# Hybrid decoder layer: the time mix's negated block inverse turned on VectorE, and output projection A taken by another order of column tiles

## The chip, the cores and the metric

One core of one Trainium2 chip runs the whole layer in one launch. The metric is the device time of one execution in microseconds. The kernel before took 2263.12 us (median of 3 runs, 2262.97 to 2263.64).

## What is computed

A sequence of 1040 tokens (16 learned meta tokens and 1024 inputs) of width 1024 goes through one layer:

```python
h = h + 0.5 * swiglu(rms_norm(h, ffn1_norm), ...)          # d_ff 2816
proj = rms_norm(h, mix_norm) @ w_in                        # q, k, v and the time mix's columns
sb = stick_breaking_attention(q, k, v)                     # 8 heads of 64
rw = rwkv7_time_mix(proj[..., 1536:], ...)                 # 8 heads of 64, a recurrence over tokens
h = h + concat([sb, rw]) @ w_out                           # the output projection
h = h + 0.5 * swiglu(rms_norm(h, ffn2_norm), ...)
out = rms_norm(h, final_norm)[:, 16:]
```

The time mix's state goes S <- S diag(w) - (S kk)(kk a)' + v k' from token to token, and a token's output is S r.

## The kernel before

**Tiles and groups.** Everything is kept transposed: channels on partitions, tokens along the free axis. The tokens are worked in two groups, A (16 meta tokens and 512 inputs) and B (512 inputs). Each fp32 operand is split into a high and a low fp32r part, and each product is three matmuls (high by high, high by low, low by high; `mm3`). A weight tile of 512 KB (eight blocks of 128 rows by 128 columns) is loaded by SyncE's queue (SP) into one of two buffers `wraw`. ScalarE (ACT) writes its high part `whi`, VectorE (DVE) its low part `wlo`, each with two buffers as well. So a tile can be split only when the tile two before it has been used up, and loaded only when the tile two before it has been split.

**The order of the work.** A planner written in the kernel (`Clock`) plays all tasks as generators against a model of the engines' costs. It issues each engine's instructions in the order in which its own clock would run them. The model counts 0.3 us of SP's time for a DMA. On the chip each engine runs its list in order, with semaphores, SP's list of DMAs too. The dense work (the FFNs and projections) is task 0 and runs through from end to end. The time mix's tasks (preparation, `lanes`, `chain`, `post`) and the attention's tasks are laid between its matmuls. Where the planner sees TensorE idle for longer than 0.45 us beside output projection A, it adds a pair of matmuls on the identity (`warm`).

**The time mix's inverse (`lanes`, line 1558).** The time mix goes by chunks of 64 tokens. There are eight units (two token groups, two halves of each, two pairs of heads), and one unit has 8 or 10 chunk and head pairs (Q). Each needs the inverse of a 64 by 64 unit triangular matrix per head and chunk. `lanes` first inverts the 16 by 16 diagonal blocks on GpSimd (POOL), one block on each partition. Its result T goes back to the matrices' layout through DRAM: one DMA `Td<-T`, and eight DMAs `t<-Td` of 8 or 10 KB that put block rows on partitions (tile t1, 128 partitions by Q by 32). A negated and turned copy goes the same way: ACT writes -T' to `lt`, one DMA writes it to Nd, and eight DMAs `tt<-Nd` put it on the diagonal of tt (128 partitions by Q by 128). Then TensorE merges 16 to 32 (matmuls `pw` and `pp`) and 32 to 64 (`pz` and `pe`). `pw` reads t1, `pp` reads tt. ACT and DVE carry the parts back into tt and t1. `chain` uses tt as the weights of `pu`.

**Output projection A (`wout`, line 2010).** It has eight column tiles m of 128 outputs and two ranges of 256 tokens, 0 and 1, hence sixteen products of 24 matmuls each. The order is given by `WOUT[0]` and a rule in `wout`: tiles 0 and 1 take both ranges; then tiles 2 to 7 take range 0; tiles 6 and 7 are kept and take range 1; then tiles 2 to 5 are loaded and split again and take range 1. It is twelve loads. Each product's result is added to the residual h on DVE, ACT squares it, and DVE adds the squares up. After the eighth product of range 0 its norm goes on (`norm_sums`, `norm_root`, `norm_end`): sums by TensorE (`nps`), a reciprocal root by DVE (`fst`), the root spread over the partitions by TensorE (`nyp`), and eight scaled and split blocks (`nf`, `nh`, `nl`) on DVE, ACT and POOL. FFN 2 begins with range 0's gate product (`pg`), which reads them. Range 1's norm follows while range 0 is in the first four gate and up products.

**The last range (`final_last`, line 2063).** The sums of the squares are matmuls too (`fss`). The loop transposes each tile into PSUM (`po`) as it is done. For the last tile (`hs`) it issues the sums of all squares but the last, then the two transposes of that tile, then the last square's sums, and then the root on DVE. DVE and ACT scale one half of the columns each (`ot`), and one DMA of 512 KB for each of two blocks of 128 tokens writes the output.

Of the kernel before, what the change touches and what calls it, by code (L numbers as in the profile page):

```python
# [7 lines left out]
F32 = mybir.dt.float32  # L8
F32R = mybir.dt.float32r
I32 = mybir.dt.int32  # L10
AF = mybir.ActivationFunctionType
# [5 lines left out]
P = 128  # L17
D = 1024
# [19 lines left out]
GB = 2  # L38
BUFS = [dict(raw=2, qs=4, kh=4, vs=2, sg=8, f=3, at=4, z=2, t=2, o=1),
        dict(raw=1, qs=4, kh=4, vs=2, sg=8, f=2, at=4, z=2, t=2, o=1)]  # L40
WOUT = ((0, 1, 2, 3, 4, 5, 6, 7, 2, 3, 4, 5), (0, 1, 2, 3, 4, 5, 6, 7))
QF = dict(ffn1=6, ffn2=4)
AHEAD = 0.1
IDLE = 0.45
# [430 lines left out]
class Ker:  # L475
# [1082 lines left out]
    def lanes(self, s, free):  # L1558


        nc, rp, dp = self.nc, self.rp, self.dp
        Q = 2 * s["NC"]
        nl, B = 8 * Q, 16
        ab = s["ab"]
        Ld, Td, Nd = (dp.tile([nl, B, B], F32, name=n, bufs=2) for n in ("Ld", "Td", "Nd"))
        blks = [(slice(B * i, B * i + B), slice(B * (i % 4), B * (i % 4) + B), slice(i * Q, i * Q + Q)) for i in range(8)]
        with self.urgent():
            for r, c, l in blks:
                nc.sync.dma_start(out=Ld[l].rearrange("l s t -> s l t"), in_=ab[r, :, c])
        yield from self.room(rp, ("lt", 1), ("T", 1), ("ltmp", 1))  # L1570
        lt = rp.tile([nl, B, B], F32, tag="lt", name="lt")
        T = rp.tile([nl, B, B], F32, tag="T", name="T")
        tmp = rp.tile([nl, 64], F32, tag="ltmp", name="ltmp")
        with self.urgent():
            nc.sync.dma_start(out=lt, in_=Ld)
        E = nc.gpsimd
        E.memset(T, 0.0)
        E.memset(T.rearrange("l i c -> l (i c)")[:, 0:B * B:B + 1], 1.0)
        for j in range(B - 1):
            m, w = B - 1 - j, j + 1  # L1580
            tv = tmp[:, 0:m * w].rearrange("l (i c) -> l i c", c=w)
            E.tensor_tensor(out=tv, in0=lt[:, j, j + 1:B].unsqueeze(2).to_broadcast([nl, m, w]),
                            in1=T[:, j, 0:w].unsqueeze(1).to_broadcast([nl, m, w]), op=ALU.mult)
            E.tensor_tensor(out=T[:, j + 1:B, 0:w], in0=T[:, j + 1:B, 0:w], in1=tv, op=ALU.subtract)
        nc.scalar.activation(lt.rearrange("l c i -> l i c"), T, AF.Copy, scale=-1.0)
        with self.urgent():
            nc.sync.dma_start(out=Td, in_=T)
            nc.sync.dma_start(out=Nd, in_=lt)
        yield lambda: free()
        yield self.after(T)  # L1590
        yield from self.room(rp, ("lr", 1), ("tt", 1), ("lw", 1))

        t1 = rp.tile([P, Q, 32], F32, tag="lr", name="t1")
        tt = rp.tile([P, Q, P], F32, tag="tt", bufs=1, name="tt")
        nc.gpsimd.memset(t1, 0.0)
        nc.gpsimd.memset(tt, 0.0)
        for r, c, l in blks:
            with self.urgent():
                nc.sync.dma_start(out=t1[r, :, r.start % 32:r.start % 32 + B], in_=Td[l].rearrange("l i c -> i l c"))
                nc.sync.dma_start(out=tt[r, :, r], in_=Nd[l].rearrange("l c i -> c l i"))  # L1600
        lw = rp.tile([P, Q * 48], F32, tag="lw", name="lw")
        w = lw[:, 0:16 * Q].rearrange("l (q i) -> l q i", i=16)
        z = lw[:, 16 * Q:48 * Q].rearrange("l (q i) -> l q i", i=32)
        g4 = [slice(32 * i, 32 * i + 32) for i in range(4)]
        up, dn = g4[0::2], g4[1::2]
        bank = (self.psc, "U", 2)
        mm = lambda out, l, r: nc.tensor.matmul(out, lhsT=l, rhs=r, start=True, stop=True)

        def U(nm, n):
            return self.psc.tile([P, 512], F32, tag="U", bufs=2, name=nm)[:, 0:n * Q].rearrange("p (q t) -> p q t", t=n)  # L1610

        yield self.need(t1, ab, bank=bank)
        pw = U("pw", 16)
        for c in range(Q):
            for i, g in enumerate(g4):
                mm(pw[g, c, :], ab[g, c, 32 * (i % 2):32 * (i % 2) + 32], t1[g, c, 0:16])
        nc.scalar.activation(w, pw, AF.Copy)
        yield self.need(w, tt, bank=bank)
        pp = U("pp", 32)
        for c in range(Q):  # L1620
            for i, g in enumerate(g4):
                mm(pp[g.start:g.start + 16, c, 0:16], w[g, c, :], tt[g, c, g.start + 16:g.stop])
        for c in range(Q):
            for g in up:
                mm(pp[g, c, 16:32], tt[g, c, g], w[g, c, :])
        for g in up:
            nc.vector.scalar_tensor_tensor(t1[g, :, 0:16], pp[g, :, 16:32], self.half[g], t1[g, :, 0:16], ALU.mult, ALU.add)
        for g in g4:
            nc.scalar.activation(tt[g.start:g.start + 16, :, g.start + 16:g.stop], pp[g.start:g.start + 16, :, 0:16], AF.Copy, scale=-1.0)

        yield self.need(t1, bank=bank)
        pz = U("pz", 32)
        for c in range(Q):
            for h in range(2):
                mm(pz[dn[h], c, :], ab[up[h], c, 32:64], t1[up[h], c, :])
        for h in range(2):
            nc.scalar.activation(z[dn[h]], pz[dn[h]], AF.Copy)
        yield self.need(z[dn[0]], z[dn[1]], tt, bank=bank)
        pe = U("pe", 32)
        for c in range(Q):  # L1640
            for h in range(2):
                mm(pe[up[h], c, :], z[dn[h], c, :], tt[dn[h], c, dn[h]])
        for h in range(2):
            nc.scalar.activation(tt[up[h], :, dn[h]], pe[up[h]], AF.Copy, scale=-1.0)
        s["tt"] = tt
# [364 lines left out]
    def wout(self, h2, n, hook, ready=None, late=False):  # L2010


        nc = self.nc
        ow = self.wcols("w_out")

        def one(m, wh, wl, i):
            cs = slice(256 * i, 256 * i + 256)
            if ready:
                yield lambda: ready(i)
            yield self.need(*[x[k][:, cs] for k in range(KT) for x in n[0:2]], bank=self.nextbank)  # L2020
            pd = self.bank("pwo")[:, 0:256]
            for k in range(KT):
                self.mm3(pd, wh[:, k, :], wl[:, k, :], n[0][k][:, cs], n[1][k][:, cs], k == 0, k == KT - 1)
                yield
            hd = h2[:, m, cs]
            with self.urgent():
                nc.vector.tensor_tensor(out=hd, in0=pd, in1=hd, op=ALU.add)
            hook(i, m)
        load = lambda m, keep=False: self.wget(ow[:, :, m * P:m * P + P], KT, P, keep)
        kept = []  # L2030
        for j, m in enumerate(WOUT[late]):
            keep = m > 5 and not late
            w = yield from load(m, keep)
            for i in (0, 1) if m < 2 or late else (int(j > 7),):
                yield from one(m, *w, i)
            if keep:
                kept.append((m, w))
            if keep and m == 7:
                for q, x in kept:
                    yield from one(q, *x, 1)  # L2040
                    self.drop(x)
# [21 lines left out]
    def final_last(self, s, h2, cs, bank, early):  # L2063
# [3 lines left out]
        for m in range(KT):  # L2067
            yield lambda: s()["k"] > min(max(m, m // 4 * 6), KT - 1)
            if m == KT - 1:
                sums = self.norm_sums(s(), 256, "fss", bank)  # L2070
                for _ in s()["last"]:
                    yield next(sums)
                last = next(sums)
                src = s()["scaled"]
            else:
                src = h2[:, m, cs]
            yield self.need(src)
            for b in range(2):
                if m % 4 == 0:
                    if m:  # L2080
                        yield self.need(bank=self.nextbank)
                    pts.append((bank if m else early)("po"))
                    self.hold(pts[-1:])
            for b in range(2):
                nc.tensor.transpose(out=pts[m // 4 * 2 + b][:, m % 4 * P:m % 4 * P + P], in_=src[:, b * P:b * P + P],
                                    identity=self.ident)
        yield last
        st, _ = yield from sums
        yield lambda: hasattr(self, "fo")
        for b in range(2):  # L2090
            ot = self.fo.tile([P, D], F32, name="ot%d" % b)
            with self.urgent():
                nc.vector.tensor_scalar(out=ot[:, 0:512], in0=pts[b], scalar1=st[:, 1, b:b + 1], scalar2=None, op0=ALU.mult)
                nc.scalar.activation(ot[:, 512:D], pts[2 + b], AF.Copy, scale=st[:, 1, b:b + 1])
                nc.sync.dma_start(out=self.out[0, 512 + cs.start + b * P:512 + cs.start + b * P + P, :], in_=ot)
        self.drop(pts)


# [435 lines left out]
```

## Time and profile before

| | |
|---|---|
| median of 3 runs | 2263.12 us |
| the profiled execution's own time | 2261.24 us |
| its span (first to last instruction) | 2259.5 us |
| TensorE busy, of the span | 2231.0 us, 99% |
| VectorE, ScalarE, GpSimd busy | 68%, 49%, 25% |
| TensorE's mean granted clock | 0.997 |

The profile is one execution. PE is TensorE's matmuls, PEld its weight loads, SPq the queue of DMAs that SyncE issues. The time of an SPq row is its issue, with what it waited for, and not the transfer. Matmuls overlap: the start of the next one tells their rate, not the duration of one. A bracket at the end of a row is the engine's idle time before it, and what ended it. All instructions carry line 104, the helper that records them, so rows are told apart by their tiles.

### The profile page before, as it was taken

Reading aid. Unit: us, or ns where it says so; the run is one execution under the profiler, and the core shown is the slowest. Engines: PE = TensorE matmul, PEld = TensorE weight load, DVE = VectorE, ACT = ScalarE, POOL = GpSimd, SP = SyncE. Lnnn points to the kernel's source line nnn. Section 1 sums busy time; section 2 is a strip of 40 time slices with the busy share of each in tenths; the row PEclk is TensorE's granted clock in tenths of the full one; section 3 lists DMA queues with packets and bytes.
Section 4 is the critical chain, followed back from the end, with each engine's and each line's share of the span. In section 5 each row is a group of like instructions: output and inputs, shape, how many; then the busy total and the mean of one; then the engine's idle time right before and its main releaser. Section 6 shows DMA issues by size and latency. Waiting matters only on the chain.

```text
span 2259.5 us, 41743 instructions
## 1 busy us (share of the span) xinstructions
PE 2231.0 (99%) x16409; PEld 1979.1 (88%) x16409; DVE 1547.4 (68%) x2633; ACT 1096.6 (49%) x2176; POOL 567.8 (25%) x722
## 2 busy tenths in 40 slices
PE   9999999999999999999999989999999999999998
PEld 8999999999878888778788988887778899899998
DVE  5887776475766745666476888557776556897774
ACT  5444444534354434554434554535665435454444
POOL 1321111013233132542011424324444001221110
PEclk9999999999999999999999999999999999999999
DMA  5543332545643233322556534233222433333332
GB/s 171 176 113 103 89 99 78 171 132 139 189 115 98 78 96 112 92 78 82 167 147 179 150 100 124 77 111 99 85 78 68 141 107 126 108 97 109 103 93 76
DMA packets 408442, 257.61 MB, mean 114 GB/s; under 512 B 44973, under 2 KB 392325, under 8 KB 408246
## 3 DMA queue, kind: packets, MB, share of 16 engines
q1 hardware_dynamic: 408246, 254.95, 38.5%
q8 instruction: 129, 2.11, 0.4%
q14 instruction: 67, 0.55, 0.1%
HBM read 220.90 MB, written 33.99 MB: 113 GB/s over the span
## 4 chain that ended last, share of the span: by engine, by line
PE 95%; DVE 3%; ACT 1%; issue 1%; DMA 0%; DVEq 0%; ACTq 0%
PE pd L104 35%; PE pu L104 22%; PE pg L104 21%; PE pwo L104 3%; PE px L104 3%; PE po L104 2%; PE pz L104 2%; PE pat L104 2%; DVE wlo L104 1%; PE pG L104 1%; PE psw L104 0%; ACT whi L104 0%; DVE nl L104 0%; PE pp L104 0%; PE pT L104 0%
## 5 line engine op out<-in xcount | busy, mean ns | idle before, releaser
L104 ACT ACTIVATE whi<-wraw 128x1024 fp32r<-128x1024 f32 x314 | 330.5, 1053 | 318.8 <-PE pd L104 209.0
L104 DVE TENSOR_TENSOR wlo<-wraw,whi 128x1024 fp32r<-128x1024 f32 (+1 forms) x312 | 399.5, 1281 | 93.7 <-ACT whi L104 87.2
L104 PE MATMUL pd<-ah,whi 128*128 128x512 f32 (+2 forms) x944 | 327.2, 347 | 2.6 <-DVE h L104 1.8
L104 PE MATMUL pd<-ah,wlo 128*128 128x512 f32 (+2 forms) x944 | 319.1, 338 | 0.0
L104 PE MATMUL pd<-al,whi 128*128 128x512 f32 (+2 forms) x944 | 318.9, 338 | 0.2
L104 PE MATMUL pd<-nh,whi 128*128 128x256 f32 (+7 forms) x648 | 210.5, 325 | 0.0
L104 PE MATMUL pu<-nh,whi 128*128 128x512 f32 (+3 forms) x576 | 205.5, 357 | 0.1
L104 PE MATMUL pd<-nl,whi 128*128 128x256 f32 (+7 forms) x648 | 204.5, 316 | 0.0
L104 PE MATMUL pd<-nh,wlo 128*128 128x256 f32 (+7 forms) x648 | 204.5, 316 | 0.0
L104 PEld LDWEIGHTS pd<-ah,whi 128*128 128x128 f32 x944 | 177.6, 188 | 27.1 <-issue 4.4
L104 PE MATMUL pu<-nl,whi 128*128 128x512 f32 (+3 forms) x576 | 197.8, 343 | 0.0
L104 PE MATMUL pu<-nh,wlo 128*128 128x512 f32 (+3 forms) x576 | 197.7, 343 | 0.0
L104 PE MATMUL pg<-nh,whi 128*128 128x512 f32 (+3 forms) x536 | 196.3, 366 | 0.6 <-ACT nh L104 0.6
L104 PEld LDWEIGHTS pd<-ah,wlo 128*128 128x128 f32 x944 | 177.6, 188 | 20.5
L104 PEld LDWEIGHTS pd<-al,whi 128*128 128x128 f32 x944 | 177.8, 188 | 17.6 <-DVE al L104 1.1
L104 POOL TENSOR_TENSOR qs<-wraw 128x512 f32<-128x512 f32 x64 | 97.7, 1530 | 373.9 <-DVE ql L104 124.6
L104 PE MATMUL pg<-nl,whi 128*128 128x512 f32 (+3 forms) x536 | 188.6, 352 | 0.9 <-DVE nl L104 0.9
L104 PE MATMUL pg<-nh,wlo 128*128 128x512 f32 (+3 forms) x536 | 188.3, 351 | 0.0
L104 POOL TENSOR_TENSOR al<-sl,ah 128x512 fp32r<-128x512 f32 (+2 forms) x45 | 71.2, 1581 | 346.1 <-ACT ah L104 336.4
L104 DVE SCALAR_TENSOR_TENSOR h<-pd,h 128x256 f32<-128x256 f32 (+1 forms) x200 | 107.6, 542 | 73.7 <-PE pd L104 71.3
L104 PEld LDWEIGHTS pd<-nh,whi 128*128 128x128 f32 (+2 forms) x648 | 120.1, 185 | 12.4 <-issue 3.1
L104 PEld LDWEIGHTS pd<-nh,wlo 128*128 128x128 f32 (+2 forms) x648 | 120.1, 185 | 8.9 <-DVE wlo L104 0.2
(395 smaller groups left out, 5657.0 us busy)
## 6 DMA issues: line engine op xcount, KB each, us to landing
wraw<-in_ffn_w_gate_dram SPq DMA_DIRECT2D x90, 512.0 KB
wraw<-in_ffn_w_up_dram SPq DMA_DIRECT2D x90, 512.0 KB
wraw<-in_ffn_w_down_dram SPq DMA_DIRECT2D x88, 512.0 KB
wraw<-in_w_in_dram SPq DMA_DIRECT2D x54, 512.0 KB
wraw<-in_w_out_dram SPq DMA_DIRECT2D x20, 512.0 KB
s<-rkvd SPq DMA_DIRECT2D x18, 256.0 KB
raw<-qkvd SPq DMA_DIRECT2D x16, 264.0 KB
raw<-qkvd SPq DMA_DIRECT2D x16, 256.0 KB
```

The lines of the kernel that those rows point to most:

```text
L104: self._c.trace(self._n, op, lambda: f(*a, **k), out, [x for x in args if isinstance(x, bass.AP)], k)
```

## The change

Three parts. In `lanes`, -T' no longer goes by way of ACT, Nd and eight DMAs: when t1 has landed, one VectorE instruction transposes its 32 by 32 blocks into z (part of the tile `lw`), and four ACT instructions copy them, negated, onto the diagonal of tt. In output projection A, tiles 0 to 3 take both ranges at once, tiles 4 to 7 take range 0, tiles 6 and 7, kept, take range 1, and only tiles 4 and 5 are loaded again: ten loads. In `final_last`, all sums and the root are issued ahead of the last tile's two transposes, and each output block goes out in two DMAs of 256 KB.

```diff
-WOUT = ((0, 1, 2, 3, 4, 5, 6, 7, 2, 3, 4, 5), (0, 1, 2, 3, 4, 5, 6, 7))
+WOUT = ((0, 1, 2, 3, 4, 5, 6, 7, 4, 5), (0, 1, 2, 3, 4, 5, 6, 7))
...
-        Ld, Td, Nd = (dp.tile([nl, B, B], F32, name=n, bufs=2) for n in ("Ld", "Td", "Nd"))
+        Ld, Td = (dp.tile([nl, B, B], F32, name=n, bufs=2) for n in ("Ld", "Td"))
...
-        nc.scalar.activation(lt.rearrange("l c i -> l i c"), T, AF.Copy, scale=-1.0)
         with self.urgent():
             nc.sync.dma_start(out=Td, in_=T)
-            nc.sync.dma_start(out=Nd, in_=lt)
...
                 nc.sync.dma_start(out=t1[r, :, r.start % 32:r.start % 32 + B], in_=Td[l].rearrange("l i c -> i l c"))
-                nc.sync.dma_start(out=tt[r, :, r], in_=Nd[l].rearrange("l c i -> c l i"))
...
+        yield self.after(t1)
+        nc.vector.transpose(out=z, in_=t1)
+        for g in g4:
+            nc.scalar.activation(tt[g, :, g], z[g], AF.Copy, scale=-1.0)
         yield self.need(t1, ab, bank=bank)
...
-            for i in (0, 1) if m < 2 or late else (int(j > 7),):
+            for i in (0, 1) if m < 4 or late else (int(j > 7),):
...
                 sums = self.norm_sums(s(), 256, "fss", bank)
-                for _ in s()["last"]:
-                    yield next(sums)
-                last = next(sums)
+
+                st, _ = yield from sums
...
-        yield last
-        st, _ = yield from sums
...
-                nc.sync.dma_start(out=self.out[0, 512 + cs.start + b * P:512 + cs.start + b * P + P, :], in_=ot)
+                for c in (slice(512, D), slice(0, 512)):
+                    nc.sync.dma_start(out=self.out[0, 512 + cs.start + b * P:512 + cs.start + b * P + P, c], in_=ot[:, c])
```

## Rows read from the trace of the kernel before

**Rows 1.** Stretches: us, busy us (instructions) of PE, PEld, DVE, ACT, POOL, clock, DMA
```profile
1252.00:1323.00 71.00, 64.16 (x696) 60.86 (x695) 57.34 (x113) 39.16 (x82) 25.13 (x45) 0.95 0.50 138
2250.00:2259.50 9.50, 2.03 (x20) 1.94 (x18) 3.48 (x12) 1.68 (x3) 0.00 (x0) 0.73 0.28 110
```

**Rows 2.** PE's waits: who waited for whom, us in total, times, longest
```profile
PE pz L104 <- DVE t L104: 4.3, 2, 3.8
PE pu L104 <- ACT us L104: 2.0, 4, 0.8
PE pwo L104 <- DVE wlo L104: 1.2, 2, 0.8
```

**Rows 3.** PE in order of time, output projection A: start, us, instruction, idle before
```profile
1288.26 0.28 PE L104 MATMUL pwo<-nh,wlo 128*128 128x256 f32 x1
1304.28 0.38 PE L104 MATMUL warm<-ident 128*128 128x128 f32 x2
1308.49 0.24 PE L104 MATMUL pz<-t,ab 32*32 32x32 f32 x2 [3.83 <-DVE t L104]
1309.17 1.06 PE L104 MATMUL pz<-t,ab 32*32 32x32 f32 x30 [0.44 <-DVE t L104]
1310.16 0.58 PE L104 MATMUL pwo<-nh,whi 128*128 128x256 f32 x1
1311.45 0.58 PE L104 MATMUL pwo<-nh,wlo 128*128 128x256 f32 x1 [0.49 <-DVE wlo L104]
...
1315.67 0.31 PE L104 MATMUL pwo<-nh,whi 128*128 128x256 f32 x1
```

**Rows 4.** SP's queue in order of time, same stretch
```profile
1286.79 0.50 SPq L104 DMA_DIRECT2D Td<-T  x1
1290.27 0.46 SPq L104 DMA_DIRECT2D Nd<-lt  x1
1290.84 2.44 SPq L104 DMA_DIRECT2D t<-Td  x5
1293.39 2.25 SPq L104 DMA_DIRECT2D tt<-Nd  x5
1299.47 1.03 SPq L104 DMA_DIRECT2D wraw<-in_w_out_dram  x2
```

**Rows 5.** ACT in order of time, same stretch
```profile
1303.40 1.06 ACT L104 ACTIVATE whi<-wraw 128x1024 fp32r<-128x1024 f32 x1 [2.90 <-DMA wraw<-in_w_out_dram]
1304.37 0.70 ACT L104 ACTIVATE nh<-nf 128x256 fp32r<-128x256 f32 x2
```

**Rows 6.** POOL in order of time: the last block of range 0's norm
```profile
1308.37 0.72 POOL L104 TENSOR_TENSOR nl<-nf,nh 128x256 fp32r<-128x256 f32 x1 [0.81 <-ACT nh L104]
```

**Rows 7.** The chain of waits, output projection B
```profile
1798.41 44.10 PE pwo L104 x378
```

**Rows 8.** Tiles tt and lt: duration ns min/median/max, first and last start
```profile
L104 ACT ACTIVATE tt<-pe x16: 358/375/428, 558.1 to 1461.5; 32x256 f32<-32x256 f32 x12, 32x320 f32<-32x320 f32 x4
L104 ACT ACTIVATE lt<-T x8: 635/646/660, 535.0 to 1438.9; 64x256 f32<-64x256 f32 x6, 80x256 f32<-80x256 f32 x2
```

**Rows 9.** DVE in order of time: the nearest and the longest instructions of such a shape
```profile
2250.46 0.35 DVE L104 TENSOR_SCALAR hs<-h2B,vec 128x256 f32<-128x256 f32 x1
1290.77 1.23 DVE L104 TENSOR_TENSOR_SCAN pe<-dec,rst 128x520 f32<-128x520 f32 x1
```

**Rows 10.** The end, in order of time: PE, DVE, SP
```profile
2251.27 0.41 PE L104 MATMUL po<-ident,hs 128*128 128x128 f32 x2
2251.53 0.50 PE L104 MATMUL fss<-ones,nsq 128*128 128x1 f32 x4
2253.64 1.41 DVE L104 TENSOR_SCALAR ot<-po,fst 128x512 f32<-128x512 f32 x2
2254.47 0.99 SPq L104 DMA_DIRECT2D out_dram<-ot  x2
```

**Rows 11.** DMA rate from 2240 to 2260, in 40 slices of 0.5 us
```profile
GB/s 0 0 0 0 0 33 0 0 0 0 0 303 381 389 389 381 254 0 0 0 0 0 0 0 0 0 0 0 0 0 188 401 410 410 401 287 0 0 0 0
```

## The prediction

> **What bounds the kernel now.** I read the page's table of engines first: TensorE is busy for 2231.0 of 2259.5 us, at a mean clock of 0.997. The change removes no product of the dense work, so it can only win what is left: 28.5 us of idle time, and stretches at the low clock. Next the busy time by stretch. The end has 9.5 - 2.03 = 7.5 us of idle TensorE, and output projection A 71.0 - 64.16 = 6.8 us, the one long stretch with a clock below 1.00 [rows 1]. In the waits of TensorE the largest entry is `pz` for t1, 4.3 us, nearly all of it one wait of 3.8; weight splits (`pwo` for `wlo`) make 1.2 us [rows 2]. So I read that stretch in order of time, engine by engine.
>
> **What happens there.** TensorE runs out of work after the `warm` pair at 1304.28, stands for 3.83 us, then 0.44 and 0.49: 4.76 us [rows 3]. Behind that come matmuls at a slower rate. From 1310.16 to 1315.67 there are 21 of them in 5.51 - 0.49 = 5.02 us, 0.239 us each; output projection B, undisturbed, runs 378 in 44.10 us, 0.117 each [rows 3, 7]. This is TensorE's lower clock of 1.2 GHz, after it had stood. It costs 5.02 - 21 x 0.117 = 2.6 us there, and about 0.5 us in the 32 small `pz` before. The hole is worth 4.76 + 3.1 = 7.8 us.
>
> Its cause is in two queues. SP issues `Td<-T` at 1286.79, then stands until 1290.27 for ACT's turned copy (`Nd<-lt`), then issues eight `t<-Td` and eight `tt<-Nd`, about 0.47 us each; only at 1299.47 does the next load of w_out follow [rows 4]. ACT's next instruction is the split of that load: it stands 2.90 us, until 1303.40 [rows 5]. Behind it in ACT's list wait the blocks of range 0's norm, and the pieces of tt and t1 that `pz` needs. So `pz` waits for DVE, DVE for ACT, ACT for a load, and the load for SP's place behind the lanes.
>
> **The change, part by part.**
>
> *SP's queue in `lanes`.* Per unit, `Nd<-lt` and eight `tt<-Nd` go. By the rows just read: the stand at `Nd`, 1290.27 - 1286.79 - 0.50 = 3.0 us, its issue of 0.46, and 8 x 0.45 = 3.6, together 7.0 us [rows 4]. The load would be issued at 1292.5 instead of 1299.5 and land 3.9 us later (1303.40 - 1299.47), near 1296.4. Without its 2.90 us stand ACT would have been ready at 1300.5, so half of the 7.0 us would do. This alone should close the hole.
>
> *Order of the tiles.* Two of twelve loads go, with their splits on ACT (1.06 us each [rows 5]) and DVE. Tiles 0 to 3 now serve two products each, 2 x 24 x 0.117 = 5.6 us per load, so loads run ahead; the second loads of 4 and 5 are wanted when 6 and 7 of range 1 run, and their buffers come free with the splits of 6 and 7. Of the 1.2 us of `pwo` waits, 0.5 is in the hole; of the other 0.75 I count half, 0.4 (bounds 0 to 0.75).
>
> The same edit takes cover away. Between the last product of range 0 and its gate stand four products, no longer six. Range 0's norm took from 1288.54 (end of its last product) to 1309.09 (last `nl`), 20.6 us [rows 3, 6]. Of this ACT's stand and split took 2.90 + 1.06 = 4.0, leaving 16.6. Four products are 11.2 us of matmuls. The whole projection took 70 us for 16 x 2.8 = 44.8; less some 9.9 us of waits and low clock, other tasks make up a quarter of TensorE's time, so the four last 11.2 / 0.745 = 15.0 us. I take 16.6 - 15.0 = 1.6, as 1.5 us, a new idle wait at `pg`. Bounds: 0 (the eight steps of the root do not wait among the preparation's scans), and 20.6 - 15.0 = 5.6 us, with which the 3.1 us of low clock would come back: 8.7.
>
> *DVE and ACT in `lanes`.* Per unit one transpose of 128x256, and four copies of 32x256 with the stride of tt, 0.375 us each like `tt<-pe`, less one `lt` of 0.646: 0.85 us more on ACT [rows 8]. The trace has no such transpose. From both sides: 0.35 us (a 128x256 instruction) and 1.23 (a scan of 128x520) [rows 9]; I take 0.4, since the element count is that of the first. Eight units: 3 us more on DVE, 7 on ACT, both idle for a third or more of the span. The new wait is the transpose's for t1's eight DMAs. Behind it on DVE are weight splits, residual adds and `chain`'s copies, and TensorE's waits for such copies were 0.8 us at most [rows 2]. Before, `pw` waited for t1 and never idled for it. Per unit 0 to 0.8 us, in all 0 to 6.4; it could also gain, as tt is ready some 4 us sooner, but no TensorE wait names that. I take 0.5 us lost.
>
> The trace cannot price the transpose; the Trainium skill's "VectorE: DVE Perf Modes", section "The three transpose paths", gives 311 ns for 128x128 bf16. By its figure an estimate is about 0.6 us for twice the columns, and the sum above would not move.
>
> *The end.* The last sums stand behind the `po` of the last tile: they start at 2251.53, that pair at 2251.27; moved ahead they gain 0.26 us, and the pair then runs beside the root, which takes until 2253.64 [rows 10]. Four DMAs for two: the last issue moves back by about 0.5 us (0.99 for two [rows 10]), but has half the bytes. Four DMAs of 256 KB just before ran at 381 to 389 GB/s, two of 512 KB at 401 to 410 [rows 11]: 0.1 us more on 1 MB. In the end the transfer is bound by the rate, and I take -0.3 for both (bounds -0.5 and +0.5).
>
> Against this edit speaks the Trainium skill, "DMA: Bandwidth & Descriptors", "Rules for kernel authors": it wants at least 1 MiB per DMA for the full rate. The trace agrees in the sign, by that twentieth.
>
> *Elsewhere.* The planner's order changes from the first unit on (from about 520 us). The waits outside this stretch and the two ends sum to some 10 us in pieces below 1 us; I take 0, with ±2.
>
> **Sum.** -7.8 - 0.4 + 1.5 + 0.5 - 0.3 = -6.5 us. Against the profiled execution's 2261.24 (span 2259.5 and 1.7 around it) this is 2254.7. The median shown is 1.9 above that execution, so 2256.6.
>
> **Rivals.**
>
> *A load still stands behind the lanes.* SP still keeps `Td`, its round trip through DRAM and eight `t<-Td`, and loads still wait for free buffers in order. For it: SP stood at other things too in this stretch. Against it: half of the 7.0 us is enough. If half the hole stays: -6.5 + 3.9 = -2.6, 2260.5.
>
> *The norm takes the hole's place.* Four products do not cover it. At the full 20.6 us the loss is 8.7 instead of 1.5: -6.5 + 7.2 = +0.7, 2263.8. For it: DVE was busy for 57.3 of 71 us there [rows 1]. Against it: the 4.0 us for the load go.
>
> *All waits of the projection go.* No norm wait, no lanes' wait, and the smaller waits of the stretch (about 1.7 in all) go too: -7.8 - 1.7 - 0.3, and 1 us from elsewhere: -10.8, 2252.3.
>
> *Slower: DVE stands for t1.* The planner puts the transpose where its model has t1 landed, with no slack; it counts a small DMA at 0.3 us of SP's time, the rows show 0.47 [rows 4]. Eight of them make it late by 8 x 0.17 = 1.4 us, in each of eight units. With the transpose and the four copies in series behind it, 0.4 + 4 x 0.375 = 1.9 us, a unit's merges come up to 3.3 us later than planned, 8 x 3.3 = 26 us. If half of that reached TensorE, 13: -6.5 - 0.5 + 13 = +6.0, 2269.1. The time is worse than before from (6.5 + 0.5) / 8 = 0.9 us of TensorE's idle time per unit, and beyond what can be told from no change from 1.4. Against it: `pw`, which needs the same data, did not idle in any unit, and DVE is idle for a third of the span.
>
> **How the numbers follow.** What a measurement of this kernel can tell from no change is about 0.2%, 4.5 us: 2258.6 to 2267.6. The forecast 0.45 and all waits going 0.13 lie below it: faster 0.58. The half hole 0.12, the norm 0.12, and the planner's order eating 3 us or more 0.08 lie within: same 0.32. DVE standing, 0.10, lies above: slower 0.10. The range reaches from all waits going with 1 us more from elsewhere, 2251, to the norm case with a little, 2265; it leaves out about 0.15.
>
> **What would show it.** Right: SP's next load of w_out directly behind eight `t<-Td`; no wait of `pz` above 1 us; the clock 1.00 in all of projection A; ten loads of w_out there; a transpose near 0.4 us; `pg` with at most 2 us ahead of it; the last `fss` ahead of the last `po`. Wrong: a wait of over 4 us at `pg` with the clock falling behind it, or DVE idle ahead of its transposes with TensorE waits for `us` of over 1 us.

## The result, and the profile after

The changed kernel takes 2269.15 us (median of 10 runs, 2267.35 to 2273.26) against 2264.15 for the kernel before in the same set: a ratio of 1.0025, 95% interval 1.0017 to 1.0033. It is slower by 5.0 us where 6.5 us less were forecast, and above the range.

Its profiled execution took 2269.35 us, near its median. That of the kernel before, 2261.24, lay 2.9 us below the median just given, so the two traces differ by 3 us more than the kernels do.

The page after: span, and busy time, share and instructions of each engine.

```profile
span 2267.6 us, 41710 instructions
PE 2239.6 (99%) x16423; PEld 1985.3 (88%) x16423; DVE 1542.4 (68%) x2639; ACT 1103.0 (49%) x2198; POOL 571.5 (25%) x722
```

TensorE is busy for 8.6 us more, with the same dense work, and idle for 28.0 us as against 28.5. What is lost is hidden in busy time: matmuls at the low clock, and `warm` matmuls (48 for 34) that the planner puts where TensorE has nothing else.

The two stretches of [rows 1] after; a third, where the clock was 1.00 in the kernel before, and the same with what lies around it (from 1215); all of output projection A with what lies around it (to 1340); and what follows (to 1450). Then the last four of these stretches of the kernel before.

```profile
1252.00:1323.00 71.00, 65.79 (x697) 62.62 (x697) 50.65 (x111) 37.97 (x86) 27.66 (x46) 0.93 0.42 120
2250.00:2267.60 17.60, 10.39 (x92) 10.13 (x90) 6.49 (x24) 7.34 (x15) 0.00 (x0) 0.83 0.32 120
1240.00:1248.00 8.00, 6.73 (x43) 6.39 (x42) 5.55 (x13) 4.38 (x11) 0.00 (x0) 0.79 0.58 180
1215.00:1252.00 37.00, 35.60 (x411) 32.60 (x410) 30.52 (x63) 19.95 (x52) 4.53 (x5) 0.95 0.45 137
1252.00:1340.00 88.00, 82.11 (x837) 78.23 (x837) 65.65 (x153) 47.30 (x113) 27.66 (x46) 0.94 0.40 114
1340.00:1450.00 110.00, 106.32 (x856) 89.53 (x856) 82.26 (x160) 56.56 (x123) 54.96 (x94) 1.00 0.36 100
```

```profile
1240.00:1248.00 8.00, 7.39 (x66) 6.72 (x64) 5.85 (x16) 4.48 (x11) 0.54 (x1) 1.00 0.62 190
1215.00:1252.00 37.00, 35.96 (x341) 33.10 (x342) 31.47 (x66) 22.20 (x58) 5.05 (x6) 1.00 0.53 158
1252.00:1340.00 88.00, 80.35 (x835) 76.35 (x833) 71.92 (x154) 49.80 (x109) 26.97 (x47) 0.96 0.45 126
1340.00:1450.00 110.00, 107.58 (x909) 90.76 (x908) 82.31 (x158) 57.03 (x124) 51.81 (x92) 1.00 0.37 103
```

From such a row I take what TensorE lost: its idle time, and (1 - clock) of the stretch. The clock is given to 0.01, so such a loss is known to some 0.4 us in 88. From 1252 to 1340 that is 7.65 + 3.5 = 11.2 us before and 5.9 + 5.3 = 11.2 after. The hole's gain is not there. From 1240 to 1248 it is 0.6 before and 1.27 + 1.68 = 3.0 after; with the neighbourhood, 1215 to 1252, it is 1.0 and 3.2.

SP's queue after, beside [rows 4]: no stand at `Nd`, no `tt<-Nd`, and the next load of w_out directly behind eight `t<-Td`, 8.3 us behind `Td` and not 12.7, where 12.7 - 7.0 = 5.7 were forecast. Two `mixd<-yt` came in between: SP now stood 3.0 us (1290.31 to 1293.28) for `yt`, as it had stood for `Nd`.

```profile
1289.77 0.54 SPq L104 DMA_DIRECT2D Td<-T  x1
1293.28 0.81 SPq L104 DMA_DIRECT2D mixd<-yt  x2
1294.18 3.73 SPq L104 DMA_DIRECT2D t<-Td  x8
1298.02 0.40 SPq L104 DMA_DIRECT2D wraw<-in_w_out_dram  x1
```

DVE, ACT and then PE, each in order of time, in the same stretch. The transpose takes 0.45 us. Read the two splits of tile 4, which is loaded a second time: the high part at 1306.74, the low part at 1317.67.

```profile
1299.20 0.45 DVE L104 STREAM_TRANSPOSE lw<-t 128x256 f32<-128x256 f32 x1 [1.43 <-DMA t<-Td]
1305.11 0.34 DVE L104 SCALAR_TENSOR_TENSOR t<-pp,half,t 32x128 f32<-32x128 f32 x1 [2.45 <-ACT tt L104]
1306.16 0.42 DVE L104 TENSOR_TENSOR h<-pwo,h 128x256 f32<-128x256 f32 x1
1306.88 1.28 DVE L104 SCALAR_TENSOR_TENSOR nf<-h,vec,ny 128x256 f32<-128x256 f32 x3 [0.29 <-ACT ny L104]
...
1316.10 0.74 DVE L104 TENSOR_TENSOR nl<-nf,nh 128x256 fp32r<-128x256 f32 x1 [0.67 <-ACT nh L104]
...
1317.67 1.20 DVE L104 TENSOR_TENSOR wlo<-wraw,whi 128x1024 fp32r<-128x1024 f32 x1
```

```profile
1299.74 1.71 ACT L104 ACTIVATE tt<-lw 32x256 f32<-32x256 f32 x4 [1.47 <-DVE lw L104]
1306.74 1.05 ACT L104 ACTIVATE whi<-wraw 128x1024 fp32r<-128x1024 f32 x1
1313.03 1.06 ACT L104 ACTIVATE whi<-wraw 128x1024 fp32r<-128x1024 f32 x1 [1.54 <-PE pwo L104]
```

```profile
1306.64 0.58 PE L104 MATMUL pwo<-nh,whi 128*128 128x256 f32 x1 [1.58 <-DVE h L104]
1312.95 0.38 PE L104 MATMUL warm<-ident 128*128 128x128 f32 x2
1313.89 0.49 PE L104 MATMUL warm<-ident 128*128 128x128 f32 x2
1315.70 0.66 PE L104 MATMUL warm<-ident 128*128 128x128 f32 x4
1318.19 0.66 PE L104 MATMUL pu<-us,tt 128*128 128x64 f32 x4 [1.83 <-ACT tt L104]
1318.69 1.09 PE L104 MATMUL warm<-ident 128*128 128x128 f32 x6
```

The waits of [rows 3] are gone, and others stand in their place. Between the two splits DVE does the blocks of range 0's norm (`nf`, `nl`), which are urgent, while a load's split has one level less. The load of tile 4 was not what was late: it was issued at 1289.31, ahead of the lanes' DMAs. Behind a stand of 1.58 us (until 1306.64) TensorE finishes tile 7's product by 1313.1; then it has a little of the time mix, 14 `warm` (2.6 us) and a stand of 1.83 us, and the next product starts at 1319.4. With all `warm` of the stretch counted as idle (18 matmuls, 3.4 us; before 6, 1.15 us) it lost 14.6 us, and before 12.3: 2.2 us more.

The two traces differ by 8.1 us (spans 2267.6 and 2259.5). Of these 2.2 lie between 1215 and 1252, 2.2 between 1252 and 1340, and 2.0 between 1340 and 1450 (3.7 idle and 6 `warm`, 1.15 us, against 2.4 and 2, 0.4). Most of the rest is scatter: from 1060 to 1080 both traces are busy alike (18.76 and 18.77 us), but the clock was 0.93 in the changed kernel's; it was 1.00 in the other, and in `e1_lanes` below, which issues the same instructions there.

### The profile page after: what moved, and what is told of

Same layout as the page of the kernel before. It is cut to its first block, busy times and chain, and to the rows that moved or that the text cites. A ratio compares the mean times of both kernels' runs of the same rounds, so it can differ in the third digit from the quotient of the medians.

```text
span 2267.6 us, 41710 instructions
## 1 busy us (share of the span) xinstructions
PE 2239.6 (99%) x16423; PEld 1985.3 (88%) x16423; DVE 1542.4 (68%) x2639; ACT 1103.0 (49%) x2198; POOL 571.5 (25%) x722
## 5 line engine op out<-in xcount | busy, mean ns | idle before, releaser
L104 DVE TENSOR_TENSOR wlo<-wraw,whi 128x1024 fp32r<-128x1024 f32 (+1 forms) x310 | 394.1, 1272 | 90.3 <-ACT whi L104 80.4
```

The source lines that it names most:

```text
L104: self._c.trace(self._n, op, lambda: f(*a, **k), out, [x for x in args if isinstance(x, bass.AP)], k)
```

## The experiments

All are ratios to the kernel before in the same set, since the chips of the sets differ by about 1 us.

**The three parts alone, and one number of the planner.** `e1_lanes` has the new `lanes` and nothing else, `e2_wout` the new `WOUT` and `m < 4`, `e3_tail` the new `final_last`. The fourth is the kernel before with

```diff
-IDLE = 0.45
+IDLE = 0.55
```

> Only the part in lanes: VectorE's transpose and ScalarE's four copies in place of Nd and its eight DMAs; output projection A and the end as before. Theory of the tiles (the loss is made by the new order of tiles in output projection A): between 2 us faster and 2 us slower than before. Theory of the lanes (the transposes and copies hold VectorE's and ScalarE's lists up): 5 to 8 us slower, with TensorE's waits behind them. Theory of chance (any change of the planner's order moves the time by several us): anything between 4 faster and 6 slower.

> Only the new order of tiles in output projection A (ten loads for twelve); lanes and the end as before. Theory of the tiles: 4 to 7 us slower than before, TensorE out of work for some 6 us while the second split of tile 4 stands behind range 0's norm on VectorE. Theory of the lanes: 0 to 6 us faster, since loads get ahead. Theory of chance: anything between 4 faster and 6 slower.

> Only the end: all sums ahead of the last tile's transposes, four DMAs for two. All theories: 0.3 to 1.0 us faster than before, the span up to 2240 us the same within 0.5 us, since nothing ahead of the end is ordered otherwise. A difference of more than 2 us would be the runs' own scatter.

> The kernel before with one number of the planner changed: it adds its pairs of matmuls on the identity beside output projection A only where it sees TensorE idle for 0.55 us and not 0.45. No part of the change is in it. Theories of the tiles and of the lanes: within 1.5 us of before. Theory of chance: 3 us or more off, either way, as the order from output projection A on is another.

Lanes: 2281.87 us, 1.0083 (1.0068 to 1.0098). Tiles: 2265.31, 1.0004 (0.9995 to 1.0012). End: 2264.64, 1.0000 (0.9991 to 1.0009). The planner's number: 2264.75, 1.0001 (0.9992 to 1.0009). So the theory of the tiles falls for the tiles alone, and the lanes lose, more than the whole change does and more than the 5 to 8 us expected. The theory of chance was not tested: the trace of `j1_idle` has the same 41743 instructions as that of the kernel before, 34 `warm` among them, in the same order on every engine. That run is the kernel before once more. Whether another order of the early work would cost as much by itself, no run here shows. The stretch of projection A in the run of the lanes alone:

```profile
1252.00:1340.00 88.00, 82.62 (x853) 77.62 (x852) 72.95 (x160) 52.18 (x118) 28.72 (x47) 0.98 0.47 132
```

It lost 5.4 + 1.8 = 7.1 us, 4.0 less than before (9.2 against 12.3 with `warm`, 3.2 less): with the old order of tiles the hole does close in part. But projection B moved. Its products, first and last start, in this run, and the loads of w_out:

```profile
L104 PE MATMUL pwo<-n2Bh,whi x128: 277/280/416, 1847.1 to 1901.7; 128*128 128x256 f32 x128
```

```profile
L104 SPq DMA_DIRECT2D wraw<-in_w_out_dram x24: 367/379/593, 1242.6 to 1891.8; - x24
```

Before, it began at 1798.4 inside FFN 2 A [rows 7], with 8 of 20 loads. Attention B ended at 1795.8 (its last write of `mixd`; 1777.4 in the run of the end alone), past the last place where the plan could still put the projection, so it came after FFN 2 A, with twelve loads.

**Is it the order of loads, or the place?** `b1_late` is `e1_lanes` with

```diff
             F["woutat"] = None
-            yield from wout(False)
+            yield from wout(True)
...
-                late = F["woutat"] is not None
+                late = True
```

and `c2_lanes_place` is `e1_lanes` with one more place, ahead of FFN 2 A's eight last down products:

```diff
+                elif poll and F.get("f2b") and "woutat" not in F:
+                    F["woutat"] = NFT
+                    yield from wout(True)
                 yield from [down(f0, f1, q) for q in range(f1 - f0)]
...
+            if f1 == NFT and poll:
+                yield from poll(NFT)
```

> The kernel before with the lanes' part of the change (as in the run of that part alone, 2281.9 us), and one thing more: where output projection B has missed its last place inside FFN 2 A, it still loads the eight tiles for both ranges each, and not twelve loads. Theory of the place (the lanes' part alone was slow because projection B came after FFN 2 A and in the order of twelve loads): its waits for weight splits go (5.8 us) and the low clock behind them (1.7), so 2274, between 2268 and 2277; the loads of w_out in the trace fall from 24 to 20. Theory of the lanes (the transposes and copies themselves cost the time, all along): 2280 to 2284, unchanged.

> The lanes' part alone (2281.9 us), with the same additional place for projection B, and nothing else. Theory of the place: FFN 2 A's last eight products (22 us) cover the norm of range 0 again, and the time falls by 13 to 17 us to 2265 to 2269. Theory of the lanes (the transposes and copies cost the time all along): 2279 to 2283.

With eight loads: 2281.03, 1.0072 (1.0058 to 1.0086). My expectation was wrong: the loads fell to 20, and the time stayed. TensorE's waits, total, times and longest, show why. Nothing was left to cover the norm of projection B, and it now waits for that.

```profile
PE nyp L104 <- DVE fst L104: 2.9, 1, 2.9
PE pu L104 <- DVE wlo L104: 2.9, 2, 1.7
...
PE nps L104 <- DVE nacc L104: 1.5, 1, 1.5
```

With the additional place, everything ahead of it issued as in the run of the lanes alone: 2272.84, 1.0037 (1.0025 to 1.0049). The place cost some 10 us (1.0083 to 1.0037). Some 8 us (0.37%) remain, and not all of them belong to the lanes: projection B is still later than in the kernel before (from 1829.1). Two of TensorE's waits between 1860 and 2000 in this run:

```profile
PE pg L104 <- DVE t4l L104: 1.8, 1, 1.8
PE pd L104 <- ACT ah L104: 1.3, 1, 1.3
```

With a third (`pu` for `wlo`, 0.7) they make 3.8 us, where the changed kernel waits 1.1 between 1800 and 2000: 2.7 us are the place once more. The changed kernel, which has projection B in its old place inside FFN 2 A (from 1807.3), does not owe its loss to it.

**The reloaded tile.** `b2_split` is the changed kernel with urgent splits for tiles that projection A loads again; `c1_split_place` adds the place above; `c4_before_split` is the kernel before with the splits; `b4_late_split` is `b1_late` with them, and `c3_split12_tail` that with the end's part. The edit of `wsplit`, which gets `now` for such a tile:

```diff
-        self.clock.ahead = True
+        self.clock.ahead = not now
...
-        self.split(hi, lo, raw, self.nc.gpsimd if self.nsplit < 3 else None)
+        with self.urgent() if now else nullcontext():
+            self.split(hi, lo, raw, self.nc.gpsimd if self.nsplit < 3 else None)
```

> The changed kernel (2269.2 us) with one thing undone in effect: in output projection A the splits of the two tiles that are loaded a second time are issued in order of need, ahead of the blocks of range 0's norm and not behind them. Theory of the end (the second low part of tile 4 stood 10 us behind norm blocks on DVE, and TensorE had only fillers): the product of tile 4 starts some 6 us earlier, few of the 14 additional warm products remain, and the time is 2264, between 2261 and 2267. Theory of the lanes (the loss is in the transposes and copies): 2269 plus or minus 1.5. If the norm then becomes the late one, the gate waits and the time stays at 2268 or more.

> The lanes' part alone with both edits of this set: eight loads for a projection B that comes late, and urgent splits of the four tiles that projection A loads a second time (twelve loads). Theory of the place: as the run with the first edit or up to 3 us better (2.7 us of waits for weight splits in projection A go), 2266 to 2274; if projection B comes inside FFN 2 A again, 2262 to 2265. Theory of the lanes: 2279 to 2284.

> The changed kernel with urgent splits of the two reloaded tiles (2276.9 us), and one place more where output projection B may come: ahead of the eight last down products of FFN 2 A, when it has missed all earlier ones. Everything ahead of that is issued in the same order. Theory of two causes (the end of projection A costs the changed kernel its 5 us, and a projection B that comes behind FFN 2 A costs another 10 or more, because nothing covers its norm): both are gone here, 2264, between 2261 and 2267. If the place is not what cost the 8 us of the run without it: 2275 to 2278. If the place is, but the end of projection A is not the cause of the changed kernel's loss: 2268 to 2271.

> The lanes' part, twelve loads in projection A with urgent splits for the four reloaded tiles (2262.4 us in the run without the end's part), and the end's part: all of the change but its order of tiles. If these add, 2262 (2260 to 2264), faster than the kernel before by 0.1%, and the order of tiles is the part of the change that loses.

> The kernel before with nothing but urgent splits for the four reloaded tiles of projection A. The hole behind the lanes (a load behind eight transfers) stays, so by the theory that the lanes' part closes it and wins 2 us net: 2264 to 2266, no better than before. If it comes to 2262 or less, it was the splits and not the lanes that made the run with both the fastest so far.

`b2_split`: 2276.92, 1.0056 (1.0043 to 1.0068), a miss, because projection B lost its place again (1842.9 to 1896.5). With the place, `c1_split_place`: 2264.50, 0.9997 (0.9989 to 1.0006), 5 us under the changed kernel (6 by the ratios), as expected, although its projection B comes later (from 1821.8) and has the waits of 3.8 us just shown. DVE and the stretch in this run: the low part starts 1.1 us behind the high one (1308.09), and the stretch lost 4.65 + 3.5 = 8.2 us, 9.4 with `warm`, where it had lost 14.6.

```profile
1309.17 1.23 DVE L104 TENSOR_TENSOR wlo<-wraw,whi 128x1024 fp32r<-128x1024 f32 x1 [0.37 <-ACT whi L104]
```

```profile
1252.00:1340.00 88.00, 83.35 (x856) 79.78 (x855) 68.74 (x154) 50.37 (x117) 29.47 (x49) 0.96 0.42 118
```

But `c4_before_split` took 2259.99, 0.9976 (0.9967 to 0.9984): urgent splits win as much without the change, against my expectation, and make a kernel that beats both. The lanes of before still hold SP until 1301.89 there, and ACT still stands 2.01 us for the load. TensorE had products meanwhile: its longest stand there is 2.04 us, and the stretch lost 4.6 + 1.8 = 6.3.

```profile
1252.00:1340.00 88.00, 83.42 (x869) 79.50 (x867) 74.84 (x165) 52.47 (x116) 31.37 (x51) 0.98 0.50 136
```

So the stretch was bound by the order of urgent work on DVE and ACT as much as by SP's queue. With the lanes, `b4_late_split` took 2262.40, 0.9993 (0.9984 to 1.0001), as expected for a projection B in its old place (from 1799.2), and `c3_split12_tail` 2265.07, 1.0001 (0.9992 to 1.0009), above the 2260 to 2264 expected: against `c4_before_split` the lanes in all units cost 0.17% and 0.25%, 4 to 6 us.

**DVE's stand for t1.** `b3_slack` is the changed kernel with

```diff
-        yield self.after(t1)
-        nc.vector.transpose(out=z, in_=t1)
+        yield self.need(t1)
+        with self.urgent():
+            nc.vector.transpose(out=z, in_=t1)
```

and the copies likewise.

> The changed kernel (2269.2 us) with the transpose placed by the planner with the slack of its other waits, and transpose and copies of tt taken with urgency. Theory of the lanes (DVE stands for t1 and ACT's copies stand in line, which makes the merges late): the stands of DVE ahead of the transposes go (1.9 us in all) and the time falls to 2264 to 2266. Theory of the end: it is not these, so 2269, between 2266 and 2272, and what differs is the planner's order.

2270.92, 1.0026 (1.0016 to 1.0037), as the changed kernel, although DVE no longer stands for t1 ahead of any transpose in its trace. The stand for t1 is not the cause.

**Which units?** On `c4_before_split` with the additional place (where projection B kept its old one), the new lanes in the last three of the eight units alone, or in the first five (`nlan` counts the calls of `lanes` from 0; where `new` is false, `lt`, `Nd` and `tt<-Nd` stay as before):

```diff
+        self.nlan = getattr(self, "nlan", -1) + 1
+        new = self.nlan > 4     # in the other kernel: < 5
```

> The kernel before with urgent splits of the reloaded tiles (2260.0 us), with the lanes' part in the last three of the eight units alone (from the one in projection A on), and the additional place for projection B, which changes nothing unless the other places are missed. Theory of the early units (the cost is the low clock at 1240 us): no fall of the clock there, and 2259 to 2261. Theory of the late units (what the transposes and copies put ahead of the merges and adds in projection A): 2262 to 2266.

> The complement: the lanes' part in the first five units alone, with the same splits and the additional place. Theory of the early units: the clock falls at 1240 us (0.8 in an 8 us window), 2262 to 2265. Theory of the late units: 2259 to 2261, whatever the clock does at 1240.

Last three: 2260.01, 0.9973 (0.9963 to 0.9984). First five, in the same set: 2267.81, 1.0009 (1.0000 to 1.0018), slower than expected. The same two stretches, of the last three, then of the first five:

```profile
1240.00:1248.00 8.00, 7.68 (x62) 7.07 (x60) 6.60 (x16) 4.07 (x12) 0.00 (x0) 1.00 0.50 153
1252.00:1340.00 88.00, 83.03 (x877) 78.61 (x876) 76.07 (x165) 52.91 (x119) 32.07 (x50) 1.00 0.48 135
```

```profile
1240.00:1248.00 8.00, 6.73 (x42) 6.27 (x42) 5.18 (x13) 3.93 (x10) 0.00 (x0) 0.79 0.67 204
1252.00:1340.00 88.00, 81.08 (x858) 77.61 (x857) 73.33 (x159) 52.10 (x116) 32.42 (x49) 0.98 0.47 131
```

The loss is in the first five units. In the unit that the prediction looked at and the two behind it the new lanes cost nothing that can be told: the clock there is 1.00 throughout, for 0.98 without them. In the five units ahead of it, all under other work and with no wait that I had listed, they cost 7.8 us. The two parts do not add up, though: new lanes in all eight units cost 4 to 6 us on the same splits, less than in these five alone. Where the first five lose, against the last three: from 1240 to 1248 2.6 us (1.3 + 1.7 against 0.3), but the other kernel stands more just beside it, and from 1215 to 1252 1.2 are left (1.4 + 1.85 against 2.1); from 1252 to 1340 3.7 (6.9 + 1.8 against 5.0); and from 1340 to 1450, of the last three, then of the first five, 4.1 (3.75 + 2.2 against 1.85):

```profile
1340.00:1450.00 110.00, 108.15 (x834) 90.47 (x835) 81.94 (x157) 56.28 (x122) 51.89 (x91) 1.00 0.36 102
1340.00:1450.00 110.00, 106.25 (x836) 89.79 (x835) 77.87 (x150) 53.68 (x117) 47.18 (x89) 0.98 0.36 102
```

These sums count idle time at the low clock twice, and the two traces differ by 6.3 us in all, so they tell where and not how much: in and behind projection A, where the fifth unit's lanes are long done. At the places of the five units themselves (545 to 1215) TensorE is idle for 3.0 us in one trace and 3.1 in the other.

## Why the prediction was wrong

**Two steps failed.** The larger is the sum for output projection A, -7.8 - 0.4 + 1.5 + 0.5 = -6.2 us: in the traces the stretch lost 2.2 us more than before. The terms follow below. The other is the one headed "Elsewhere": "The planner's order changes from the first unit on ... I take 0, with ±2." In the changed kernel's trace 2.2 us more are lost from 1215 to 1252 and 2.0 from 1340 to 1450. By themselves the lanes' part in the first five units cost 7.8 us on the kernel with urgent splits, and in all eight 4 to 6. (The 8.4 us of the run with the additional place, 0.37% of 2265, hold some 2.7 of projection B's place.) What is shown of it begins at 1240. These are ACT, then PE, of the changed kernel:

```profile
1241.03 2.00 ACT L104 ACTIVATE whi<-wraw 128x1024 fp32r<-128x1024 f32 x2
1243.05 0.27 ACT L104 ACTIVATE rsv<-pu 64x128 f32<-64x128 f32 x1
```

```profile
1242.12 0.44 PE L104 MATMUL px<-rsv,bg 128*128 128x64 f32 x2 [0.44 <-DVE rsv L104]
1243.38 0.88 PE L104 MATMUL px<-rsv,bg 128*128 128x64 f32 x6 [0.83 <-ACT rsv L104]
```

In the new order two weight splits stand ahead of the copy that `chain` waits for, and after stands of 0.44 and 0.83 us the clock falls (0.79). Of the ten kernels with the new lanes in the early units all show a fall there (0.79 to 0.90) but `b3_slack`, which places them otherwise and takes as long in all; none of the six without them does. These six lose 1.0 to 2.2 us from 1215 to 1252 all the same, so the order at 1240 explains 1 to 2 us. That what is lost behind 1252 follows from the order too is argued only, and whether the lanes' instructions matter in it or any other order would do the same stays open.

**The hole, -7.8: 0 gained, and 2.2 lost.** Its mechanism was half right. SP no longer stands for `Nd`, though it stands as long for `yt`, and `pz` no longer waits. "This alone should close the hole" holds with the old order of tiles, at 3 to 4 us and not 7.8, since other stands and low clock stayed. In the changed kernel none of it is left: with four products behind range 0, two need a second load whose split stands behind the norm. I had priced the buffers of these two tiles and not the queue of their splits on DVE. And "their buffers come free with the splits of 6 and 7" holds only for `wraw`: the buffers of the split parts come free with the products of 6 and 7, and the high part of tile 5 waited for `pwo` until 1313.03. `c1_split_place` shows what this queue cost the changed kernel: with urgent splits the stretch lost 9.4 us instead of 14.6, and the whole kernel was 5 to 6 us faster. But the kernel before gained as much from them (`c4_before_split`), so the queue was there already; with urgent splits on both sides the change still costs 4.5 us, 2.7 of them by projection B's place. That `c4_before_split` loses most of the hole with SP's queue as it was shows that the load's place was one of two causes.

**The norm's cover, +1.5: 0.** The norm took from 1297.3 (range 0's last product) to 1317.4 (the last `nl`, on POOL), 20 us and not 16.6, but `pg` did not wait: the last two products were later still. The norm set the time in another way, ahead of the splits.

**`pwo` waits, -0.4.** `pwo` for `wlo` is gone from the list, but `pwo` for `h` rose from 0.4 to 1.8 us: the residual add at 1306.16 stood behind `t<-pp`, which waited 2.45 us for ACT.

**DVE and ACT in `lanes`, +0.5.** The rows of the transposes in the changed kernel, and what DVE's idle time ahead of them waited for (us, times):

```profile
L104 DVE STREAM_TRANSPOSE lw<-t x8: 431/442/511, 544.4 to 1454.2; 128x256 f32<-128x256 f32 x6, 128x320 f32<-128x320 f32 x2
  DMA t<-Td: 1.9, 2
```

0.44 us for 0.4 forecast. The Trainium skill's "VectorE: DVE Perf Modes", "The three transpose paths", has only 128x128 in bf16; the estimate of 0.6 us from it was too high. DVE stood for t1 in two units, 1.9 us in all, where my slower rival had 3.3 in each. That rival's time, 2269.1, was met by chance, and its mechanism did not happen.

**The end, -0.3: 0.0.** The last `fss` moved ahead of the last `po`, as said. From `hs` to the end of the span is 8.9 us (2258.71 to 2267.6) against 9.1 before, less than the runs can tell, and the part alone measured 1.0000.

**The order of tiles** costs 1.1 us by itself, not to be told from none. On top of the lanes it looks like a gain, 2272.84 to 2269.15, but the first of these also has projection B later, which costs as much; in the stretch itself the lanes alone lost 9.2 us, and with the new order of tiles 14.6.

## What to carry to other kernels

Where one planner orders all the work, a local change is a change of every order behind it: price it by that too, test it by putting it into a part of its places, and look into the trace whether a run meant as another order is one. A wait that is removed returns as whatever stands next in the same stretch; look for it in low clock and filler work, which count as busy. And before mending a queue, ask whether the work that waits had to be queued so: a level of urgency on the splits of four tiles won here what the change did not.

## What the runs showed of the hardware

- Short stands can cost more in clock than in time. After 0.44 and 0.83 us of idle time, 1240 to 1248 ran at 0.79: 1.7 us lost, more than the stands themselves. But the same stands do not always do it: between 512 and 528 all sixteen profiles stand 1.0 us in the same instructions, and ten of them showed a fall of the clock there (0.89).
- One profile is good for some 3 us here. `j1_idle` and the kernel before are the same instructions in the same order, and their traces span 2263.0 and 2259.5 us. Up to 528 us all kernels issue the same instructions; idle time there was 4.8 to 5.7 us in ten profiles and 6.2 to 7.1 in six.
- The last 1 MB, in four DMAs of 256 KB, went at 380 to 383 GB/s, where two of 512 KB had 401 to 410 [rows 11]. The four issues took 1.79 us, and the part changed nothing that can be measured.
